# A two-half decoder trunk: where the second half's four delta heads get their buffers and their projections

## The chip, the cores and the metric

The kernel runs on one core of a Trainium2 chip. The metric is the device time of one execution in microseconds (us); less is better. Before the change three runs gave a median of 2281.3 us (2279.24 to 2283.44).

## What is computed

The input x is 1024 tokens of width 1024 in fp32. Two residual layers follow one another; after each mixer and after each MLP stands a layernorm of `alpha * x + result`. Cut to what matters here:

```python
def hybrid_mixer(x, w_in, ...):                       # layer 0
    proj = x @ w_in
    qa, ka, va, qkv_b, z, beta_logit, a_logit = split_cols(proj, HYB_SPLITS)
    o_a = sliding_window_attention(rope(qa), rope(ka), va, sinks)      # 8 heads of 64, 2 kv heads, window 128
    qb, kb, vb = split(silu(causal_dwconv(qkv_b, conv_w)))             # 4 delta heads of 128, 4 taps
    o_b = gated_delta_rule(l2_normalize(qb), l2_normalize(kb), vb, g, beta)   # chunks of 64, state carried
    o_b = o_b * rsqrt(mean(o_b ** 2) + eps) * norm_w * silu(z)
    return concat([o_a, o_b]) @ w_out
def recurrent_mixer(x, ...): ...                      # layer 1: conv, RG-LRU, gelu gate, two projections
def sqrelu_mlp(x, w1, w2): return relu(x @ w1) ** 2 @ w2
for layer in range(2):
    x = layer_norm(alpha * x + (hybrid_mixer, recurrent_mixer)[layer](x))
    x = layer_norm(alpha * x + sqrelu_mlp(x))
```

## The kernel before, in words

**Products.** A product of fp32 accuracy is made of three TensorE products of a faster 32-bit format: both operands are split into a high part h and a low part l, and `mm3` (L359) adds h·h, h·l and l·h in PSUM. A weight block of 128x1024 is loaded by SyncE's DMA queue into one of three `ws` buffers, its h is cast by ScalarE (every fifth by VectorE) into `wh`, and VectorE subtracts to get `wl` (`wblock`, L349; `split`, L343). Activations lie split in granules of 128x2048 (`gran`, a pool of 14); an `ActT` is the transposed activation of one half as four granules: quads 0 and 1 of h and of l.

**Halves and order.** The 1024 tokens are worked on as two halves c = 0 and c = 1 of 512 tokens. Each half is a generator `stream(c)` (L1329): hybrid mixer, output projection `hout` with layernorm (`mix_out`), MLP (`w1`, `w2`), recurrent mixer, MLP. The long weight products in it are the *fillers*: each `yield` releases three TensorE matmuls. The chains of short, dependent steps are *mixers*, generators too, put on a list by `spawn`: the delta heads (`head_mid`, L944), the attention blocks (`attn_preps`, `attention`), `delta_scalars`, layernorms, loads. The loop at L1355 writes TensorE's one fixed order while the program is built: a modelled clock says when a mixer's next inputs are there; if they are, its step comes next, otherwise three matmuls of a stream's filler. A generator that must wait for a buffer or a flag yields `BLOCK`. If no stream has a filler to give, the modelled clock is simply moved on, and the mixer's next step follows with nothing between. The other engines work in the order in which their instructions were issued at that build, one after the other.

**Buffers of the chains.** Besides granules there are rings of 128x512 tiles: `t` with 11, `s` with 10 and `f` with 4. A delta head keeps its q, k, v and its chain's tiles in one ring (`r`) until its end, and `need(r, n)` waits for n free tiles.

**The delta heads** are started in `hybrid` (L1246). `head_front` (L911) makes k, q and v of a head: product from `hin_fm` into PSUM, ScalarE copies it into an `f` tile beside three columns of the tokens before (`halo`), a four-tap convolution (`conv4`: one ScalarE step, three VectorE steps) and silu. `head_z` (L932) makes z, silu'd and split into quad 1 of `oT`. `head_mid` then runs the chain: transposes, Gram matrices, the inverse in levels of 32x32 matmuls, the scan over chunks, a norm, and the product with z into `oT`. In half c = 0 the heads take the rings t and s in turn, so two chains run at a time; in half c = 1 all four take ring t, one after the other, and each front waits for the ring. The z of a head is made behind the front of the next. Half 2's x is loaded (`load_x`) after the first two z of half 1. `q_proj` (L760) copies q into a granule of its own, which `attn_prep` (L796) reads; `mix_out` of half 1 keeps gamma and beta of its layernorm in four tiles of ring s, half 2 in ring t (`load_gb`, L438). `straight` (L553), one of the MLP's two ways to hold its hidden tiles, takes eight tiles of ring t or s.

In the profile L178 is the line through which all instructions of VectorE, ScalarE, GpSimd and the DMA queues go, L206 that of matmuls and L210 that of transposes; in the changed file they are L179, L207 and L211. `mm` are PSUM tiles of weight products, `mx` those of the chains' steps.

Of the kernel before, what the change touches and what calls it, by code (L numbers as in the profile page):

```python
# [13 lines left out]
ALU = mybir.AluOpType  # L14
# [15 lines left out]
FW = 528  # L30
LN_EPS = 1e-5
# [182 lines left out]
def trunk(ctx: ExitStack, tc, I, out):  # L214
# [223 lines left out]
    def load_gb(which, r):  # L438
        g = [ts(r) for _ in range(4)]
# [11 lines left out]
    def layernorm(yg, ls, which, r, yT, res, each=None):  # L451
        yield from need(r, 4)
# [12 lines left out]
        def norm(n, i):  # L465
# [8 lines left out]
            if (n, i) == halves[-1]:  # L474
                free(r, *g)
# [53 lines left out]
    def mlp(layer, c, yT, yg, ls, res, tail=False):  # L529
# [23 lines left out]
        def straight(e, done):  # L553
            j, i = divmod(e, 2)
            yield from wait(lambda: either(8))
            ring = either(8)
            own = [(ts(ring, F32R), ts(ring, F32R)) for _ in range(4)]
# [10 lines left out]
            for half in range(2):  # L568
# [13 lines left out]
                if half == 1:  # L582
                    free(ring, *(z for hl in own for z in hl))
                    if done:
                        res["n"] = NT
# [174 lines left out]
    def q_proj(c, x, st, oT):  # L760
        ps = yield from proj_tm([I["hin_q"][i] for i in range(4)], x, 512)
        st["qg"] = gran()
        for n in range(NT):
            oT.quad(0, n)
            S.copy(st["qg"][:, n * CH:(n + 1) * CH], ps[n])
# [30 lines left out]
    def attn_prep(c, n, st, tl, o):  # L796
        q, kr = v4(st["qg"][:, n * CH:(n + 1) * CH]), st["k"][n]
# [113 lines left out]
    def head_front(c, h, x, d, r):  # L911
        for j, name in enumerate("kqv"):
            yield from need(r, 1)
            yield from need("f", 2)
            raw, y, u = tl("f"), ts("f"), ts(r)
            ps = yield from proj_fm(I["hin_fm"][h * 4 + j], x)
            i = h * 3 + j
# [4 lines left out]
            S.copy(raw[:, 3:515], ps)  # L922
            if c == 0:
                S.copy(halo[:, i, :], raw[:, 512:515])
# [7 lines left out]
    def head_z(h, x, oT, d):  # L932
        yield from need("f")
        z = ts("f")
        ps = yield from proj_fm(I["hin_fm"][h * 4 + 3], x)
        S.activation(z, ps, AF.Tanh, scale=0.5)
        V.scalar_tensor_tensor(z, z, 1.0, ps, ALU.add, ALU.mult)
        S.copy(oT.h(4 + h), z)
        V.tensor_tensor(oT.l(4 + h), z, oT.h(4 + h), ALU.subtract)
        free("f", z)  # L940
# [3 lines left out]
    def head_mid(c, h, st, d, oT, r):  # L944
# [151 lines left out]
        yield from wait(lambda: "z" in d)  # L1096
# [6 lines left out]
        V.tensor_tensor(z, oT.h(4 + h), oT.l(4 + h), ALU.add)  # L1103
# [400 lines left out]
```

## Time and profile before

| | |
|---|---|
| median of three runs | 2281.3 us |
| profiled execution, its time | 2280.57 us |
| its span (first to last instruction) | 2278.7 us |
| granted TensorE clock, mean | 0.991 |
| TensorE busy | 2216.7 us |
| VectorE (DVE) busy | 1545.9 us |
| ScalarE (ACT) busy | 1049.1 us |
| moved by DMA | 332.22 MB |

The first layer's mixers of both halves lie in the first 500 us of the span; half 1's first MLP begins at about 463 us. The windows of the trace give, for a stretch of the span, the busy time of each engine, the granted clock (1.00 is full speed) and the share of time that the DMA engines were busy. The timeline gives single instructions; in brackets stands how long the engine had been idle before one, and whose instruction ended that.

### The profile page before, as it was taken

The numbers are of one execution on the slowest core, as the hardware profiler recorded it, in microseconds if no ns is written. First come the engines' busy times: TensorE is split into PE (matmuls) and PEld (weight loads), VectorE is DVE, ScalarE is ACT, GpSimd is POOL, SyncE is SP. The second block draws the span as 40 slices with busy tenths as digits, with TensorE's granted clock in tenths as the row PEclk, the third lists the DMA queues.
The fourth block names the chain that finished last, engine by engine and source line by source line (L and its number), as shares of the span: only waits on it lengthen the run. The fifth ranks groups of instructions, "written<-read, shape, count | busy, mean of one in ns | idle before, by whom it ended". The sixth has DMA issues, their size and how long they took to land.

```text
span 2278.7 us, 31897 instructions
## 1 busy us (share of the span) xinstructions
PE 2216.7 (97%) x12436; PEld 1790.4 (79%) x12436; DVE 1545.9 (68%) x2809; ACT 1049.1 (46%) x1874; POOL 28.9 (1%) x56
## 2 busy tenths in 40 slices
PE   8999989999999999999999999999999999999997
PEld 7767866778878887888888878878788887888886
DVE  7787684766645666596567898685565656776477
ACT  5465444434332344454344577373434444444442
POOL 0000000000000000000000000000000000000000
PEclk9999999999999999999999999999999999999999
DMA  4121221266778666677764343322533443454341
GB/s 165 61 78 39 94 67 45 74 175 178 216 213 225 196 211 200 210 241 229 226 216 149 128 138 105 136 79 97 180 107 121 139 148 123 155 166 148 120 163 69
DMA packets 87064, 332.22 MB, mean 146 GB/s; under 512 B 9600, under 2 KB 9984, under 8 KB 78720
## 3 DMA queue, kind: packets, MB, share of 16 engines
q1 hardware_dynamic: 73808, 275.32, 35.2%
q0 software_dynamic: 4608, 33.56, 7.8%
q10 hardware_dynamic: 8496, 21.30, 2.7%
q8 instruction: 97, 1.59, 0.3%
q14 instruction: 55, 0.45, 0.1%
HBM read 321.75 MB, written 75.50 MB: 174 GB/s over the span
## 4 chain that ended last, share of the span: by engine, by line
PE 85%; DVE 9%; ACT 3%; DMA 1%; issue 1%; ACTq 0%; DVEq 0%; SPq 0%
PE mm L206 66%; PE mx L206 17%; DVE g L178 3%; DVE wl L178 2%; PE mx L210 2%; DVE s L178 1%; DMA ws<-w 1%; ACT g L178 1%; ACT wh L178 1%; ACT s L178 1%; DVE t L178 1%; DVE f L178 1%; ACT f L178 0%; ACT t L178 0%; DVE lnw L178 0%
## 5 line engine op out<-in xcount | busy, mean ns | idle before, releaser
L206 PE MATMUL mm<-g,wh 128*128 128x512 f32 x2816 | 883.7, 395 | 3.6 <-DVE g L178 3.0
L178 DVE TENSOR_TENSOR wl<-ws,wh 128x1024 fp32r<-128x1024 f32 (+1 forms) x444 | 538.3, 1212 | 396.1 <-ACT wh L178 391.8
L178 ACT CAST wh<-ws 128x1024 fp32r<-128x1024 f32 (+1 forms) x356 | 371.5, 1044 | 705.8 <-PE mm L206 605.3
L206 PEld LDWEIGHTS mm<-g,wh 128*128 128x128 f32 x2816 | 521.6, 188 | 113.4 <-DVE g L178 5.1
L206 PE MATMUL mm<-g,wl 128*128 128x512 f32 x1408 | 549.5, 390 | 0.5 <-DVE wl L178 0.5
L206 PE MATMUL mm<-wh,s 128*128 128x512 f32 x1152 | 376.6, 393 | 0.7 <-DVE g L178 0.7
L206 PEld LDWEIGHTS mm<-g,wl 128*128 128x128 f32 x1408 | 264.7, 188 | 57.0 <-DVE wl L178 1.0
L206 PEld LDWEIGHTS mm<-wh,s 128*128 128x128 f32 x1152 | 216.3, 188 | 46.7 <-ACT s L178 1.1
L206 PE MATMUL mm<-wh,g 128*128 128x512 f32 (+1 forms) x768 | 239.3, 383 | 6.6 <-ACT wh L178 6.4
L206 PE MATMUL mm<-wl,s 128*128 128x512 f32 x576 | 224.3, 389 | 0.0
L206 PE MATMUL mx<-wh,s 128*128 128x512 f32 x576 | 187.8, 392 | 1.2 <-DVE s L178 1.2
L206 PEld LDWEIGHTS mm<-wh,g 128*128 128x128 f32 x768 | 143.0, 191 | 33.8 <-ACT wh L178 6.4
L178 ACT CAST s<-g 128x512 fp32r<-128x512 f32 x172 | 104.7, 622 | 105.2 <-PE mm L206 53.7
L178 DVE TENSOR_TENSOR s<-g,s 128x512 fp32r<-128x512 f32 x172 | 116.1, 685 | 44.7 <-ACT s L178 44.7
L206 PE MATMUL mm<-wl,g 128*128 128x512 f32 (+1 forms) x384 | 144.1, 375 | 0.2 <-DVE wl L178 0.2
L206 PEld LDWEIGHTS mx<-wh,s 128*128 128x128 f32 x576 | 108.1, 188 | 24.1 <-DVE s L178 2.0
L206 PEld LDWEIGHTS mm<-wl,s 128*128 128x128 f32 x576 | 108.3, 188 | 20.9
L206 PE MATMUL mx<-wl,s 128*128 128x512 f32 x288 | 112.1, 389 | 0.0
L178 DVE CAST wh<-ws 128x1024 fp32r<-128x1024 f32 x88 | 60.4, 686 | 73.0 <-PE mm L206 66.3
L178 DVE TENSOR_TENSOR g<-g,mm 128x512 f32<-128x512 f32 x136 | 89.1, 682 | 14.6 <-PE mm L206 14.2
L178 ACT ACTIVATE g<-mm 128x512 f32<-128x512 f32 x100 | 59.3, 593 | 73.0 <-PE mm L206 73.0
L206 PEld LDWEIGHTS mm<-wl,g 128*128 128x128 f32 x384 | 73.3, 191 | 11.7 <-DVE wl L178 0.6
(231 smaller groups left out, 2401.3 us busy)
## 6 DMA issues: line engine op xcount, KB each, us to landing
ws<-w SPq DMA_DIRECT2D x232, 512.0 KB, 3.3
ws<-t SPq DMA_DIRECT2D x96, 512.0 KB, 3.3
t<-w POOLq DMA_DIRECT2D x32, 1024.0 KB, 9.1
ws<-hin_fm SPq DMA_DIRECT2D x32, 512.0 KB, 3.3
t<-w SPq DMA_DIRECT2D x16, 1024.0 KB, 6.7
t<-t SPq DMA_DIRECT2D x16, 1024.0 KB, 6.5
ws<-rin SPq DMA_DIRECT2D x32, 512.0 KB, 3.3
ws<-hout SPq DMA_DIRECT2D x16, 512.0 KB, 3.4
```

Source lines behind the costliest of these rows:

```text
L178: r = f(*a, **k)
L206: ins = self.pe.matmul(out, lhsT, rhs, start=start, stop=stop, skip_group_check=fresh)
L210: return self._pe(self.pe.transpose(out, x, ident), out, [x], 0.00042 * 2 * out.shape[-1])
```

## The change

- `SHARED = (3,)`: head 3's k, q and v blocks, and the z blocks of all four heads, are multiplied with x of both halves at once (`proj_fm` with `also`), in half 1's stream; 25 blocks of `hin_fm` are loaded and split in place of 32. For heads 0 to 2 of half 2, k, q and v are made by `fronts` as fillers of stream 1.
- `park` copies such a raw product out of PSUM with ScalarE into a tile `r` (two buffers) and stores it with SyncE's queue in DRAM (`parked_i`, 128x512). `head_front` and `head_z` of half 2 load it from there into an `f` tile, once it is parked.
- The heads of half 2 take the rings t and s in turn and are a mixer of their own (`heads`, spawned), no part of the stream.
- z of half 1 goes unsplit into one granule `zg`; in half 2 it is split into `oT` as before. All four z come after the four fronts.
- `q_proj` of half 2 splits q into the quads of `oT`, and `attn_prep` adds h and l again; half 1 keeps its granule.
- gamma and beta of half 1's first layernorm take a granule in place of four s tiles; `straight` may take two granules where no ring has eight tiles.
- x of half 2 is loaded from the start of half 1 on, and freed when both halves have used it (`drop`).

```diff
+SHARED = (3,)
-    def proj_fm(src, x, bank=None):
+    def proj_fm(src, x, bank=None, also=None):
         wh, wl = wblock(src)
-        ps = (bank or mm_ps)()
+        xs = [x] if also is None else [x, also]
+        ps = [(bank or mm_ps)() for _ in xs]
         for k in range(KT):
             b, c = divmod(k, 4)
-            mm3(ps, wh[b][:, c * P:(c + 1) * P], wl[b][:, c * P:(c + 1) * P], x.h(k), x.l(k), k == 0, k == KT - 1)
-            if k < KT - 1:
-                yield
-        return ps
+            for i, z in enumerate(xs):
+                mm3(ps[i], wh[b][:, c * P:(c + 1) * P], wl[b][:, c * P:(c + 1) * P], z.h(k), z.l(k), k == 0, k == KT - 1)
+                if k < KT - 1 or z is not xs[-1]:
+                    yield
+        return ps[0] if also is None else ps
...
+            if c:
+                V.tensor_tensor(qs, *q, ALU.add)
+                q = qs
             rope(qs, q, 4, n, a, b)
...
+    def park(i, ps):
+        t = dpool.tile([P, CH], F32, name=f"parked_{i}", tag=f"parked_{i}")
+        o = clk.tile("r", 2, wpool.tile([P, 512], F32, tag="r", name=nm("r"), bufs=2))
+        S.copy(o, ps)
+        DS.dma_start(t, o)
+        parked[i] = t
...
     def head_front(c, h, x, d, r, also=None):
         for j, name in enumerate("kqv"):
+            i = h * 3 + j
+            b = h * 4 + j
+            yield from wait(lambda: c == 0 or b in parked)
             yield from need(r, 1)
             yield from need("f", 2)
             raw, y, u = tl("f"), ts("f"), ts(r)
-            ps = yield from proj_fm(I["hin_fm"][h * 4 + j], x)
-            i = h * 3 + j
+            if c:
+                DS.dma_start(raw[:, 3:515], parked[b])
+            else:
+                ps = yield from proj_fm(I["hin_fm"][b], x, also=also)
+                if also is not None:
+                    park(b, ps[1])
+                    ps = ps[0]
...
     def head_mid(c, h, st, d, oT, r):
-        yield from wait(lambda: "z" in d)
+        yield from wait(lambda: "z" in d and (("l", 1) in oT.g or rings["g"] >= 2))
+        oT.quad(1, 0)
...
+        def fronts(h):
+            for j in range(3):
+                ps = yield from proj_fm(I["hin_fm"][h * 4 + j], x)
+                park(h * 4 + j, ps)
+                yield UNIT
...
+        def heads():
+            for h in range(4):
+                if c == 0 and h in SHARED:
+                    yield from wait(lambda: "x" in sts[1])
+                yield from head_front(c, h, x, d[h], rs[h % 2], both if h in SHARED else None)
+                yield from wait(lambda: h - st.get("scan", 0) < 2)
+                spawn(head_mid(c, h, st, d[h], oT, rs[h % 2]))
+                if h == 0 and c == 0:
+                    yield from q()
+            if c:
+                yield from wait(lambda: "ln0" in sts[0])
+                yield from need("g", 2)
+                oT.quad(1, 0)
+            else:
+                yield from need("g", 1)
+                zg.append(gran())
+            for h in range(4):
+                yield from head_z(c, h, x, oT, d[h], both)
+        if c == 0:
+            yield from heads()
+            x.free()
+        else:
+            spawn((r if r is not UNIT else lambda: 0.0) for r in heads())
             yield from q()
+            yield UNIT
+            for h in range(1, 4):
+                if h not in SHARED:
+                    yield from fronts(h)
+        drop()
...
-        yield from hybrid(c, xT, oT, st[c], ("t", "s") if c == 0 else ("t",))
+        yield from hybrid(c, xT, oT, st[c], ("t", "s"))
         yield from mix_out(I["hout"], oT, lambda n: I["x"][c * CH + n * P:c * CH + (n + 1) * P, :], 0,
-                           "s" if c == 0 else "t", s, st[c]["t"], lambda: c == 0 or "m7" in sts[0])
+                           "g" if c == 0 else "t", s, st[c]["t"], lambda: c == 0 or "m7" in sts[0])
```

More of the change, by code (lines that the diff above doesn't have):

```diff
@@ L438, in load_gb @@
     def load_gb(which, r):
-        g = [ts(r) for _ in range(4)]
+        if r == "g":
+            q = gran()
+            g = [q[:, i * 512:(i + 1) * 512] for i in range(4)]
+        else:
+            g = [ts(r) for _ in range(4)]
         for i in range(4):
@@ L554, in straight @@
             j, i = divmod(e, 2)
-            yield from wait(lambda: either(8))
+            yield from wait(lambda: either(8) or rings["g"] >= 2)
             ring = either(8)
-            own = [(ts(ring, F32R), ts(ring, F32R)) for _ in range(4)]
+            if ring:
+                own = [(ts(ring, F32R), ts(ring, F32R)) for _ in range(4)]
+                held = [z for hl in own for z in hl]
+            else:
+                ring, held = "g", [gran(F32R) for _ in range(2)]
+                own = [tuple(z[:, i * 512:(i + 1) * 512] for z in held) for i in range(4)]
             for f in range(4):
@@ L1259, in q @@
         def q():
-            yield from need("g", 3)
+            yield from need("g", 3 - c)
             yield from q_proj(c, x, st, oT)
```

96 lines of the change are left out of this document (54 added, 42 removed).

## The prediction

> **What bounds the kernel now.** First the page: how full TensorE is, and whose chain ended last.
>
> ```profile
> span 2278.7 us, 31897 instructions
> ...
> PE 2216.7 (97%) x12436; PEld 1790.4 (79%) x12436; DVE 1545.9 (68%) x2809; ACT 1049.1 (46%) x1874; POOL 28.9 (1%) x56
> ...
> PE 85%; DVE 9%; ACT 3%; DMA 1%; issue 1%; ACTq 0%; DVEq 0%; SPq 0%
> ```
>
> TensorE is busy 97%, and the change leaves its matmuls alone in number, so all there is to win is its 2278.7 - 2216.7 = 62 us of idleness, and matmuls that ran slowly. Second the windows, which say where these lie; the columns are busy time and instructions of PE, PEld, DVE, ACT and POOL, then granted clock, DMA share and GB/s.
>
> ```profile
> 60.00:120.00 60.00, 57.62 (x823) 42.38 (x821) 42.75 (x130) 24.95 (x77) 0.10 (x1) 1.00 0.17 54
> 120.00:180.00 60.00, 55.49 (x331) 41.92 (x331) 52.14 (x164) 38.78 (x113) 0.51 (x5) 1.00 0.27 82
> 180.00:240.00 60.00, 57.80 (x809) 40.41 (x807) 43.82 (x121) 34.07 (x103) 0.00 (x0) 1.00 0.16 47
> 240.00:310.00 70.00, 68.97 (x482) 58.03 (x481) 51.97 (x172) 31.14 (x95) 0.00 (x0) 1.00 0.26 83
> 310.00:366.00 56.00, 45.05 (x465) 28.71 (x465) 32.61 (x100) 28.77 (x85) 0.00 (x0) 0.82 0.17 58
> 366.00:430.00 64.00, 64.00 (x297) 45.79 (x296) 32.34 (x79) 26.64 (x69) 0.00 (x0) 1.00 0.18 59
> 430.00:500.00 70.00, 66.09 (x572) 51.72 (x571) 53.36 (x130) 35.66 (x73) 1.75 (x2) 0.95 0.45 131
> ```
>
> One window stands out: from 310 to 366 us TensorE idles 56 - 45.05 = 10.95 us, and its clock is 0.82 where it is 1.00 around it. Third the timeline of TensorE there (start, duration, operation, in brackets the idle time before and its releaser); mx are steps of chains, mm are weight products, the fillers.
>
> ```profile
> 307.42 0.45 PE L206 MATMUL mx<-t 32*32 32x32 f32 x32
> 307.80 0.73 PE L206 MATMUL mm<-g,wh 128*128 128x512 f32 x2
> ...
> 308.60 0.62 PE L206 MATMUL mm<-g,wh 128*128 128x512 f32 x2
> ...
> 309.29 0.62 PE L206 MATMUL mm<-g,wh 128*128 128x512 f32 x2
> ...
> 316.79 0.45 PE L206 MATMUL mx<-t 32*32 32x32 f32 x32
> 318.07 0.45 PE L206 MATMUL mx<-t 32*32 32x32 f32 x32 [0.82 <-DVE t L178]
> 319.38 0.45 PE L206 MATMUL mx<-t 32*32 32x32 f32 x32 [0.86 <-DVE t L178]
> ...
> 323.53 1.97 PE L206 MATMUL mx<-g,vraw 128*64 128x512 f32 x2 [1.68 <-DVE g L178]
> ...
> 330.61 1.07 PE L206 MATMUL mx<-g,vraw 128*64 128x512 f32 x2 [0.40 <-DVE g L178]
> ...
> 340.91 1.08 PE L206 MATMUL mx<-t,t 64*64 64x64 f32 x8 [2.13 <-DVE asc L178]
> ...
> 360.54 1.16 PE L206 MATMUL mx<-kT,g 64*128 64x128 f32 x16
> ...
> 364.96 0.48 PE L206 MATMUL mm<-wh,g 128*128 128x512 f32 x1
> ```
>
> Up to 316.79 us fillers lie between chain steps and hide them; from there to 364.96 us, 48.2 us long, stands a bare run without one. A step of 0.45 us waits 0.82 us for DVE, and the same pair of 128x512 matmuls takes 1.97 us at one place and 1.07 at another. The idle and slow parts together: 10.95 + 0.18 x 45.05 = 19.1 us.
>
> **The change part by part.** (1) *The bare run.* Before, TensorE's order at its start (mm the last filler, mx_..<-t head 0's levels in half 2, mx<-csb and vraw the attention):
>
> ```order
> L206 MATMUL mm_3659<-g_2006,wh_3655 128x512
> L206 MATMUL mm_3659<-g_2005,wl_3656 128x512
> L206 MATMUL mx_3692<-t_3388 32x32 x16
> L206 MATMUL mx_3710<-t_3388 32x32 x16
> L206 MATMUL mx_3729<-t_3388 32x32 x16
> L210 MATMUL mx_3748<-csb,g_146 128x128 x2
> L210 MATMUL mx_3748<-csb,g_147 128x128 x2
> ```
>
> And in the changed kernel the same levels, between products of `hout`:
>
> ```order
> L207 MATMUL mm_486_3651<-wh_491_3657,g_106_756 128x512
> L207 MATMUL mx_493_3676<-t_464_3492 32x32 x16
> L207 MATMUL mm_487_3652<-wh_491_3657,g_105_755 128x512
> L207 MATMUL mm_487_3652<-wl_492_3658,g_105_755 128x512
> L207 MATMUL mm_487_3652<-wh_491_3657,g_106_756 128x512
> L207 MATMUL mm_488_3653<-wh_491_3657,g_105_755 128x512
> L207 MATMUL mm_488_3653<-wl_492_3658,g_105_755 128x512
> L207 MATMUL mm_488_3653<-wh_491_3657,g_106_756 128x512
> L207 MATMUL mm_489_3654<-wh_491_3657,g_105_755 128x512
> L207 MATMUL mm_489_3654<-wl_492_3658,g_105_755 128x512
> L207 MATMUL mm_489_3654<-wh_491_3657,g_106_756 128x512
> L207 MATMUL mx_494_3703<-t_464_3492 32x32 x16
> ```
>
> Nine fillers now lie between two levels: three start 0.69 us after the three before (308.60, 309.29), so nine take 2.1 us against a wait of 0.8 to 1.0. The bare run's loss goes: -19.1 us; at least -10.95, if the clock falls there as well.
>
> The row has a clock of 0.82 though its longest wait is 2.13 us. The Trainium skill's page "TensorE: Matmul & The Clock Gate" (Part 1: The HAM clock gate) says that the clock halves after an idle window of about 3.4 us; by that rule no slow clock should be here and the term would be 10.95 us. The row contradicts it, and I keep 19.1.
>
> (2) *The first layernorm of half 1.* Today it loses time at its transposes and the first `w1` product:
>
> ```profile
> 457.76 1.91 PE L210 MATMUL mx<-csb,g 128*128 128x128 f32 x16
> 461.92 1.71 PE L210 MATMUL mx<-csb,g 128*128 128x128 f32 x8 [2.25 <-DVE g L178]
> 463.30 0.80 PE L206 MATMUL mm<-g,wh 128*128 128x512 f32 x1
> 465.77 0.79 PE L206 MATMUL mm<-g,wh 128*128 128x512 f32 x1 [1.67 <-DVE g L178]
> ```
>
> With its window (70 - 66.09 = 3.9 idle, 0.05 x 66.09 = 3.3 slow) it costs 7.2 us. In the changed kernel the same place reads on TensorE (csb,g the transposes, kT attention scores, mm_4564 the last parked product of head 2, mm_4829 the first of `w1`):
>
> ```order
> L207 MATMUL mm_4564<-g_345,wl_4561 128x512
> L211 MATMUL mx_4731<-csb,g_3644 128x128 x4
> L211 MATMUL mx_4741<-csb,g_3644 128x128 x4
> L211 MATMUL mx_4751<-csb,g_3644 128x128 x4
> L211 MATMUL mx_4758<-csb,g_3644 128x128 x4
> L211 MATMUL mx_4786<-csb,g_3645 128x128 x4
> L211 MATMUL mx_4796<-csb,g_3645 128x128 x4
> L211 MATMUL mx_4806<-csb,g_3645 128x128 x4
> L211 MATMUL mx_4813<-csb,g_3645 128x128 x4
> L207 MATMUL mm_4829<-g_4694,wh_4825 128x512
> L207 MATMUL mm_4829<-g_4695,wh_4825 128x512
> L207 MATMUL mm_4829<-g_4694,wl_4826 128x512
> L207 MATMUL mx_4833<-kT_4184,g_146 128x128
> ```
>
> All eight transposes now come in one piece, and in DVE's order layernorm, attention of half 2 and the convolutions of heads 1 and 2 stand mixed. From the filler 123 before these transposes to the last split of the layernorm DVE has 136 instructions. The groups by form up to 715 us, the last column but two the mean ns:
>
> ```profile
> L178 DVE TENSOR_TENSOR wl<-ws,wh 128x1024 fp32r<-128x1024 f32 x82 | 100.2, 1222 | 55.0 <-ACT wh L178 53.9
> L178 DVE SCALAR_TENSOR_TENSOR f<-f,sm,f 128x512 f32<-128x512 f32 x72 | 53.4, 744 | 6.0 <-ACT f L178 5.3
> ...
> L178 DVE CUSTOM_DVE_ANT_0 g<-mx,csb 128x256 f32<-128x256 f32 x56 | 20.5, 419 | 1.8 <-PE mx L206 1.7
> ...
> L178 DVE TENSOR_TENSOR hsc<-hsc 128x4 f32<-128x4 f32 x80 | 12.6, 159 | 3.5 <-ACT t L178 1.8 <-ACT s L178 0.3
> ...
> L178 DVE TENSOR_TENSOR g<-mx,g 128x512 fp32r<-128x512 f32 x16 | 10.8, 684 | 10.8 <-ACT g L178 10.8
> ...
> L178 DVE TENSOR_TENSOR g<-g,s 128x512 f32<-128x512 f32 x14 | 9.2, 684 | 0.0
> ```
>
> 6 splits x 1.222 = 7.3; 17 convolution steps x 0.744 = 12.6; 14 layernorm halves and 9 splits x 0.684 = 15.7; 12 masks x 0.419 = 5.0; 29 small ones x 0.159 = 4.6; the other 49 take at most 0.684 each, 33.5 us, by kind about 20. Together about 65 us. TensorE has 123 fillers x 0.23 = 28 us there and 53 short rows, each between a score matmul (1.16 us for eight, 0.145) and four transposes (1.91 for sixteen matmuls, four such, 0.48): 8 to 25 us, by kind 17; together 45. So TensorE could wait 65 - 45 = 20 us if DVE arrived without any lead, and 7.2 if it is like today. I take the middle, 14: **-7.2 + 14 = +6.8**.
>
> (3) *Heads 1 and 2 of half 2 elsewhere* have three to six fillers (0.7 to 1.4 us) between steps, against a level's wait of 0.82 to 0.86: between 0 and +6, I take +2.
>
> (4) *Half 1.* Head 3's k, q, v and all z blocks serve both halves (seven loads and splits fewer), half 1's z isn't split, and the second products fill. Its windows from 60 to 240 us hold 2.38 + 4.51 + 2.20 = 9.1 us of idleness: between -4.5 and 0, I take -1.5. q's two additions more in half 2 fall under the count of (2).
>
> (5) *DRAM.* Sixteen products are copied by ACT, stored and loaded again through SP. SP's rows at heads 1 and 2 of half 2 (ws weight blocks, parked the stores, f<-parked the loads):
>
> ```order
> L179 DMA parked_4292<-r_4293 128x512
> L179 DMA ws_4823<-w_0 128x1024
> L179 DMA f_4296<-parked_4292 128x512
> L179 DMA parked_4373<-r_4374 128x512
> L179 DMA f_4377<-parked_4373 128x512
> L179 DMA parked_4419<-r_4420 128x512
> L179 DMA ws_4951<-w_0 128x1024
> L179 DMA ws_5017<-w_0 128x1024
> L179 DMA f_4423<-parked_4419 128x512
> ```
>
> ```profile
> L178 ACT ACTIVATE g<-mm 128x512 f32<-128x512 f32 x100 | 59.3, 593 | 73.0 <-PE mm L206 73.0
> ...
> ws<-hin_fm SPq DMA_DIRECT2D x32, 512.0 KB, 3.3
> ...
> out<-g SPq DMA_DIRECT2D x16, 256.0 KB, 2.1
> ```
>
> A load waits on SP for its store, and weight blocks queue behind it. One round trip is 0.6 + 2.1 + 3.3 = 6.0 us (a read of 512 KB as bound for 256). A block of `w1` behind it is needed some 120 fillers, 27 us, later: 0. DMA share there is 0.17 to 0.45: no contention.
>
> Sum: -19.1 + 6.8 + 2 - 1.5 = -11.8 us on the profiled execution's 2280.6, so 2268.8; the median of the runs is 0.7 higher, so **2269.5 us**.
>
> **The rivals.** *Nearly all is kept*: DVE enters the layernorm with a lead and loses 7.2 us as today, (3) costs nothing: -19.1 - 1.5 = -20.6, 2260.7 us. For it: DVE is busy only 32.34 of the 64 us after the bare run. Against: the 20 us counted in (2).
> *DVE takes it back*: it has no lead, 20 us in (2): -19.1 - 7.2 + 20 + 2 = -4.3, 2277.0 us, no change that can be told (0.2%, 4.6 us, is about what a measurement of this kernel can tell). For it: at 430 to 500 us DVE was busy 53.36 of 70 with one chain, and now has two. Against: today's loss there is 7.2.
> *The round trips stand in DVE's queue* and it ends slower. A convolution's first step waits on DVE for its load; behind it in the same queue stand the layernorm's splits, which `w1` waits for. If DVE has caught up when it comes there, it idles up to 6.0 us a product, for six of them, in a stretch where DVE is the bound. Against: with a backlog of DVE they are hidden. It decides from 4.3 + 4.6 = 9 us of such waits, two round trips; with three, 18 us on -4.3: 2295.
>
> **How the numbers follow.** The forecast 0.48, nearly all kept 0.18, taken back 0.19, round trips 0.15. Faster by over 0.2%: 0.66; within: 0.19; slower: 0.15. The range runs from a little beyond the kept case, 2256 (both waits of (4) and half of today's 7.2 gone as well), to 2286, halfway into the round trips' case.
>
> **What would show it.** Right: no stretch at head 0 of half 2 without fillers and the clock near 1.00 there; one hole of 10 to 18 us at the first transposes before `w1`, ended by DVE. The second rival: that hole near 20 us and DVE full before it. The third: DVE idle on DMA f<-parked. Wrong altogether: half 1's loss grows by more than 5 us, or weight splits waiting for DMA ws.

## The result, and the profile after

| | before | after |
|---|---|---|
| median of four runs each | 2280.27 us (2279.17 to 2283.44) | 2300.97 us (2299.31 to 2302.48) |
| span of the profiled execution | 2278.7 us | 2298.1 us |
| granted clock, mean | 0.991 | 0.988 |

After over before is 1.0088, with a 95% interval of 1.0071 to 1.0106: the change makes the kernel about 20 us slower. The forecast was 2269.5 us, in a range that ended at 2286: wrong in sign and outside the range.

The page of the changed kernel begins with its busy times; further down it gives the shares of the chain that ended last.

```profile
span 2298.1 us, 31959 instructions
...
PE 2225.6 (97%) x12436; PEld 1795.7 (78%) x12436; DVE 1540.1 (67%) x2801; ACT 1041.2 (45%) x1868; POOL 28.5 (1%) x56
...
PE 86%; DVE 7%; ACT 3%; DMA 2%; issue 1%; DVEq 0%; ACTq 0%; SPq 0%
PE mm L207 67%; PE mx L207 18%; DVE g L179 3%; PE mx L211 2%; DVE wl L179 1%; DVE s L179 1%; ACT g L179 1%; DVE f L179 1%; ACT s L179 1%; DMA f<-parked 1%; DMA ws<-xT 0%; ACT wh L179 0%; DMA ws<-w 0%; ACT f L179 0%; DMA parked<-r 0%
```

The matmuls are as many as before (12436) and VectorE, ScalarE and GpSimd are each a little less busy, yet the span is 19.4 us longer. DMA has gone from 1% to 2% of the chain, and beside the weight blocks (`ws<-w`) three kinds of transfer are named in it: loads of parked products, stores of them, and loads of x (`ws<-xT`). None of the three had a term above zero in the prediction.

Where the time lies, the windows say. First the changed kernel, then those windows of the kernel before that the prediction did not show (columns as there: busy time of PE, PEld, DVE, ACT, POOL, then granted clock, DMA share, GB/s).

```profile
0.00:60.00 60.00, 46.79 (x240) 40.64 (x241) 38.41 (x97) 30.06 (x76) 0.44 (x7) 0.94 0.56 188
60.00:310.00 250.00, 239.49 (x2302) 178.89 (x2301) 146.91 (x451) 107.66 (x316) 0.91 (x9) 0.98 0.15 50
310.00:366.00 56.00, 53.70 (x415) 44.39 (x414) 46.76 (x129) 23.52 (x73) 0.00 (x0) 1.00 0.37 128
366.00:430.00 64.00, 64.00 (x482) 51.02 (x481) 43.57 (x122) 21.77 (x51) 0.00 (x0) 1.00 0.28 91
430.00:560.00 130.00, 116.83 (x1119) 82.40 (x1118) 95.72 (x248) 69.89 (x185) 3.40 (x4) 0.95 0.50 143
560.00:760.00 200.00, 198.39 (x1222) 159.10 (x1222) 126.48 (x297) 80.45 (x176) 8.40 (x12) 1.00 0.70 206
760.00:1480.00 720.00, 713.79 (x3174) 587.08 (x3173) 502.88 (x692) 351.09 (x503) 15.38 (x24) 1.00 0.60 188
1480.00:1560.00 80.00, 72.39 (x315) 58.74 (x314) 60.02 (x91) 52.08 (x79) 0.00 (x0) 0.91 0.25 84
```

```profile
0.00:60.00 60.00, 53.38 (x285) 46.41 (x286) 43.07 (x111) 31.63 (x79) 0.75 (x10) 1.00 0.46 161
60.00:310.00 250.00, 239.89 (x2442) 182.74 (x2440) 190.68 (x585) 128.93 (x387) 0.61 (x6) 1.00 0.22 67
...
430.00:560.00 130.00, 126.09 (x967) 100.84 (x966) 93.89 (x225) 60.70 (x136) 4.23 (x5) 0.97 0.54 155
560.00:760.00 200.00, 200.00 (x1389) 160.90 (x1388) 110.77 (x241) 62.26 (x121) 9.55 (x13) 1.00 0.75 216
760.00:1480.00 720.00, 711.86 (x3166) 585.63 (x3165) 519.05 (x732) 364.00 (x523) 13.77 (x22) 1.00 0.58 183
1480.00:1560.00 80.00, 74.63 (x335) 60.68 (x334) 59.66 (x81) 51.08 (x81) 0.00 (x0) 0.98 0.26 86
```

Busy time times granted clock is the work that TensorE got done, in us at full speed; idle time and slow clock are taken out of it together. The table gives it for the kernel before and, for the others, how much more or less they did in the same window (each figure rounded to a tenth before it is subtracted; the last three columns are experiments that come below):

| window | before | after minus before | h_before_x_early | d_same_products | dks4_equal_products |
|---|---|---|---|---|---|
| 0 to 60 | 53.4 | -9.4 | -11.3 | -0.1 | -0.3 |
| 60 to 310 | 239.9 | -5.2 | -16.1 | +4.2 | +4.2 |
| 310 to 430 | 100.9 | +16.8 | +0.9 | +9.5 | +13.4 |
| 430 to 560 | 122.3 | -11.3 | +0.4 | -30.1 | +3.1 |
| 560 to 760 | 200.0 | -1.6 | 0.0 | -1.4 | -3.4 |
| 760 to 1480 | 711.9 | +1.9 | +1.5 | +1.4 | -13.9 |
| 1480 to 1560 | 73.1 | -7.2 | -1.3 | -7.3 | +2.3 |
| sum | | -16.0 | -25.9 | -23.8 | +5.4 |
| its span minus before's | | +19.4 | +22.8 | +21.7 | -5.5 |

Each sum has the size of its span's difference; the rest is what the clock's second digit leaves (0.005 of 720 us is 3.6 us in the longest window). By 60 us the changed kernel and a_no_load, b_two_hops and c_ln_light of below, whose orders are still the same on every engine there, have done 44.0, 41.6, 41.1 and 41.5 us: a difference of up to 3 us in one window of single profiles says nothing. So four places matter. The bare run gained 16.8 us, as forecast. The start lost 9.4 + 5.2 = 14.6, half 1's first layernorm 11.3, and a place in the second layer 7.2.

**The start.** TensorE in the changed kernel stands still for 6.44 us at the delta scalars' cumulative sum; the kernel before has no wait there.

```profile
39.15 1.04 PE L207 MATMUL mx<-dsc,csb 128*128 128x16 f32 x4 [6.44 <-DVE dsc L179]
```

The chain that leads to it (start, duration, piece) goes through loads of half 2's x, one after the other:

```profile
18.02 3.87 DMA ws<-xT
...
23.89 3.86 DMA ws<-xT
...
29.83 3.65 DMA ws<-xT
...
34.15 1.29 DVE g L179 x2
...
39.01 0.10 DVE dsc L179
```

Each load is followed by a split on ScalarE and VectorE; `dsc`, the small steps of the decay scalars, stand between the splits in VectorE's fixed order, and so wait for DMAs that have nothing to do with them. The bracket names VectorE; the chain shows that a DMA held VectorE up.

**The layernorm of half 1.** The chain from 430 us on:

```profile
430.64 0.48 ACT r L179
431.14 2.01 DMA parked<-r
...
433.57 3.38 DMA parked<-r
437.01 3.46 DMA f<-parked
440.58 0.73 ACT f L179
...
450.34 0.59 ACT r L179
450.94 2.34 DMA parked<-r
453.29 4.98 DMA f<-parked
458.36 0.73 ACT f L179
```

Two passages through DRAM lie on this chain. The second is one product's round trip: 8.0 us from ScalarE's copy out of PSUM to ScalarE's first convolution step (450.34 to 458.36). The first, 9.9 us (430.64 to 440.58), holds two products: the store at its head is that of the product before, whose load waits for it in SP's queue, and the next store stands behind that load. The product convolved at 440.58 was copied out at 432.91, 7.7 us earlier. From 459.11 to 477.96 the chain is VectorE's alone: it had waited 2.40 us for ScalarE's step at 458.36, and from 459 to 478 us it is busy 18.79 of 19 us.

TensorE idles 13.2 us of the 130 there, in pieces. The longest stands before transposes of head 1 of half 2 (`csb,s`); the hole of 10 to 18 us at the transposes before `w1` (`csb,g`), which the prediction named as its sign, isn't there:

```profile
435.89 0.63 PE L211 MATMUL mx<-csb,s 128*128 128x128 f32 x4 [3.78 <-DVE hsc L179]
...
470.76 3.58 PE L211 MATMUL mx<-csb,g 128*128 128x128 f32 x16 [1.68 <-DVE g L179]
...
476.56 0.50 PE L207 MATMUL mm<-g,wh 128*128 128x512 f32 x1 [1.71 <-DVE g L179]
```

**The second layer.** In its mixer one chain step waits 6.30 us for VectorE:

```profile
1497.86 1.11 PE L211 MATMUL mx<-csb,g 128*128 128x128 f32 x4 [6.30 <-DVE g L179]
```

The diff does not touch that mixer. TensorE's order there differs all the same, presumably because the clock modelled at the build arrives with other values. Which versions have this wait is told at the last experiment.

### The profile page after: what moved, and what is told of

Same layout as the page of the kernel before. It is cut to its first block, busy times and chain, and to the rows that moved or that the text cites. A ratio compares the mean times of both kernels' runs of the same rounds, so it can differ in the third digit from the quotient of the medians.

```text
span 2298.1 us, 31959 instructions
## 1 busy us (share of the span) xinstructions
PE 2225.6 (97%) x12436; PEld 1795.7 (78%) x12436; DVE 1540.1 (67%) x2801; ACT 1041.2 (45%) x1868; POOL 28.5 (1%) x56
## 4 chain that ended last, share of the span: by engine, by line
PE 86%; DVE 7%; ACT 3%; DMA 2%; issue 1%; DVEq 0%; ACTq 0%; SPq 0%
PE mm L207 67%; PE mx L207 18%; DVE g L179 3%; PE mx L211 2%; DVE wl L179 1%; DVE s L179 1%; ACT g L179 1%; DVE f L179 1%; ACT s L179 1%; DMA f<-parked 1%; DMA ws<-xT 0%; ACT wh L179 0%; DMA ws<-w 0%; ACT f L179 0%; DMA parked<-r 0%
## 5 line engine op out<-in xcount | busy, mean ns | idle before, releaser
L179 DVE TENSOR_TENSOR wl<-ws,wh 128x1024 fp32r<-128x1024 f32 (+1 forms) x437 | 529.6, 1212 | 375.9 <-ACT wh L179 371.0
L179 ACT CAST wh<-ws 128x1024 fp32r<-128x1024 f32 (+1 forms) x350 | 364.8, 1043 | 656.1 <-PE mm L207 567.2
L207 PE MATMUL mm<-wh,g 128*128 128x512 f32 (+1 forms) x896 | 284.0, 387 | 7.6 <-ACT wh L179 6.5
L207 PE MATMUL mm<-wh,s 128*128 128x512 f32 x896 | 287.5, 390 | 1.4 <-DVE g L179 1.4
L207 PEld LDWEIGHTS mm<-wh,g 128*128 128x128 f32 x896 | 167.0, 191 | 39.7 <-ACT wh L179 6.5
L207 PEld LDWEIGHTS mm<-wh,s 128*128 128x128 f32 x896 | 168.2, 188 | 37.1 <-DVE g L179 2.3
L207 PE MATMUL mm<-wl,s 128*128 128x512 f32 x448 | 174.3, 389 | 0.0
L207 PE MATMUL mm<-wl,g 128*128 128x512 f32 (+1 forms) x448 | 169.7, 379 | 0.3 <-DVE wl L179 0.3
L207 PEld LDWEIGHTS mm<-wl,s 128*128 128x128 f32 x448 | 84.1, 188 | 17.2
L179 DVE TENSOR_TENSOR g<-g,mm 128x512 f32<-128x512 f32 x136 | 89.3, 683 | 11.4 <-PE mm L207 10.9
L207 PEld LDWEIGHTS mm<-wl,g 128*128 128x128 f32 x448 | 85.7, 191 | 13.5 <-DVE wl L179 0.6
```

The source lines that it names most:

```text
L179: r = f(*a, **k)
L207: ins = self.pe.matmul(out, lhsT, rhs, start=start, stop=stop, skip_group_check=fresh)
```

## The experiments

Theories at the outset: **TRIP**, the round trips of heads 1 and 2 of half 2 lie on the path; **DVE**, VectorE has too much work at the layernorm, as term (2) said; **START**, loading half 2's x from the start delays half 1. Later: **CROWD**, half 2's chains run in the layernorm's place; **MEET**, the layernorm meets half 2's attention; **MASK** against **KEPT**, whether what late loading of x wins early is given back at the layernorm or stays. All ratios are to the kernel before, with their 95% interval; after's is 1.0088 [1.0071, 1.0106].

### a_no_load, b_two_hops, c_ln_light, d_x_late: one cost at a time

```diff
 a_no_load, in head_front of half 2
+                if h in (1, 2):
+                    nc.gpsimd.memset(raw[:, 3:515], 0.25)
+                    ...
+                else:
+                    DS.dma_start(raw[:, 3:515], parked[b])
```

> Leaves out the six loads of heads 1 and 2 of half 2 from DRAM (their convolutions run on a constant that GpSimd writes; the stores stay; TensorE's order is row for row that of the changed kernel). Theory TRIP (store and load lie on the chain that TensorE waits for, at 431 to 441 and 451 to 458 us of the changed kernel's trace): 8 to 15 us faster than the changed kernel, the hole before the transposes at 435.9 us gone. Theory DVE (in that stretch VectorE simply has more work than TensorE): 0 to 2 us faster.

```diff
 b_two_hops, in head_front of half 2
+                if h in (1, 2):
+                    hop = dpool.tile([P, CH], F32, name=f"hop_{b}", tag=f"hop_{b}")
+                    nc.sync.dma_start(hop, parked[b])
+                    nc.sync.dma_start(raw[:, 3:515], hop)
```

> Sends the same six products through DRAM twice (store, copy from DRAM to DRAM, load), TensorE's order unchanged. TRIP: each of the two trips on the chain grows by one more transfer of 256 KB, 2 to 3.5 us each: 4 to 8 us slower than the changed kernel. DVE: 0 to 1 us slower.

```diff
 c_ln_light, in layernorm
+                if r == "g":
+                    ...
+                else:
                     V.tensor_tensor(a, a, g[i], ALU.mult)
                     V.tensor_tensor(a, a, g[2 + i], ALU.add)
```

> Leaves out the multiplication by gamma and the addition of beta for seven of the eight half tiles of half 1's first layernorm (14 VectorE instructions, 14 x 0.61 us from start to start = 8.5 us less for VectorE), TensorE's order unchanged. TRIP: 0 to 2 us faster than the changed kernel. DVE: 6 to 9 us faster.

```diff
 d_x_late
-            spawn(load_x(1, xTs[1]))        # in stream, at the start of half 1
                 if h == 0 and c == 0:
                     yield from q()
+                    spawn(load_x(1, xTs[1]))
```

> Half 2's x is loaded after half 1's q product instead of from the start on; the planner's order changes behind it. Theory START (the four loads and sixteen splits of x in the first 40 us hold up the decay scalars): the wait of 6.4 us and the slow clock at 33 to 45 us go, 7 to 10 us faster there, and 4 to 10 us faster in all. Rival: the same splits only fall into the dense stretch of half 1's heads and come back there: the start is faster, the whole within 3 us.

Measured: a_no_load 2294.16 us, 1.0059 [1.0044, 1.0074]; b_two_hops 2307.38, 1.0117 [1.0102, 1.0132]; c_ln_light 2302.15, 1.0094 [1.0079, 1.0109]; d_x_late 2293.81, 1.0063 [1.0046, 1.0080]. TensorE's order in a, b and c is, row for row, that of the changed kernel. VectorE's and ScalarE's is not: it differs in places, from 361 us on in a, from 421 us in c and from 425 us in b, until about 510 us. So these runs carry some reordering beside the cost that they change. The window from 430 to 560 us, of a, b and c in that order:

```profile
430.00:560.00 130.00, 121.61 (x1180) 86.45 (x1179) 88.35 (x247) 69.32 (x186) 3.40 (x4) 0.99 0.45 131
```

```profile
430.00:560.00 130.00, 112.14 (x1077) 79.18 (x1076) 94.11 (x242) 69.36 (x186) 3.34 (x4) 0.92 0.48 144
```

```profile
430.00:560.00 130.00, 116.37 (x1112) 82.43 (x1110) 90.04 (x225) 69.20 (x181) 3.40 (x4) 0.92 0.48 142
```

Without the six loads TensorE does 121.61 x 0.99 = 120.4 us of work there, with them 111.0, with one hop more 103.2. The kernel follows: 6.8 us faster without, 6.4 slower with a further hop. That is TRIP's way in both, within its 4 to 8 us for b, but less than its 8 to 15 for a: about 1.1 us a product. TensorE's idle time in the window is 8.4 us without the loads, 13.2 with them and 17.9 with one hop more. The wait of 3.78 us before head 1's transposes is gone without the loads and grows to 5.98 with the hop; it is 5.38 in c_ln_light too, whose trips are those of the changed kernel, so this one hole alone proves nothing. The waits of that stretch name the engine (total, times, longest us), first in the changed kernel, then with one hop more; without the loads ScalarE has no such wait:

```profile
ACT f L179 <- DMA f<-parked: 8.6, 4, 2.7
```

```profile
ACT f L179 <- DMA f<-hop: 7.4, 4, 2.7
```

(Of the 8.6 us, 1.5 are head 3's product; with the hop that one waits 1.7.) It is ScalarE that waits, since the convolution's first step is its own. Its own waits hardly grow with the hop, though, while TensorE's do: what a trip costs is passed on through the engines' orders, and the traces don't split it by product. Behind the first of these steps (440.58) stand in ScalarE's order the copy of the next product out of PSUM (441.81), four steps of a delta chain (445.31) and the cast of a weight block (449.38).

DVE, as term (2) had counted it, falls: c_ln_light takes 14 of VectorE's layernorm instructions away, 14 x 0.684 = 9.6 us, and gains nothing where DVE had said 6 to 9 us; the window has 5.7 us less VectorE work and no more TensorE work than after. But these 14 run from 421 to 431 us in the changed kernel, ahead of the stretch from 459 to 478 us in which VectorE is full. Of that stretch c says little: VectorE is busy 17.62 of the same 19 us in it. (The memset gives GpSimd six instructions more, so a's 6.8 us carries that too.)

d_x_late gains 7.2 us, within START's 4 to 10, but its plan has 24 matmuls fewer (12412). In before's chain 26 fillers take 5.90 us, 0.227 each, so 24 are 5.4 us. It had to be asked again, below.

### e_direct, k5_hold: take heads 1 and 2 out of the way

```diff
 e_direct: no trip for heads 1 and 2 of half 2; product and convolution in the stream
-            if c:
+            if c and h not in (1, 2):
                 DS.dma_start(raw[:, 3:515], parked[b])
...
+            if c and h in (1, 2):
+                S.copy(raw[:, 3:515], ps)
...
+            mixer(heads((0,), False))
             yield from q()
...
+            yield from heads((1, 2), False)
+            mixer(heads((3,)))
```

> Heads 1 and 2 of half 2 take k, q and v straight from PSUM into their tiles, in the stream, as every head of the kernel before did; both rings, head 0's and head 3's parked products and all z stay as changed; the reference is computed in full. TRIP: as much faster than the changed kernel as without the six loads, 5 to 8 us. Rival: fronts that wait for a ring stop the stream again, TensorE gets bare stretches, and the gain is under 3 us.

```diff
 k5_hold: heads 1 to 3 of half 2 wait until half 1's first layernorm is done and the
 head before in their ring has ended; z head by head
+                if c and h:
+                    yield from wait(lambda: st.get("mids", 0) >= h - 1)
+                    yield from wait(lambda: phase[0] >= 1)
                 yield from head_front(...)
...
+                if c and h:
+                    if h == 1:
+                        yield from wait(lambda: "ln0" in sts[0])
+                        yield from need("g", 2)
+                        oT.quad(1, 0)
+                        yield from head_z(c, 0, x, oT, d[0], both)
+                    yield from head_z(c, h, x, oT, d[h], both)
```

> Heads 1 to 3 of half 2 start only when half 1's first layernorm is done (so that w1 products lie between their steps), a head's front waits until the head before it in its ring has ended, and z of half 2 is loaded head by head; everything else as changed. Theory CROWD (the round trips cost only because layernorm and heads 1 and 2 stand together with few fillers between): the loss at 430 to 510 us (18.8 us above the work of TensorE itself, against 7.7 in the kernel before) falls to 8 to 11, 8 to 11 us faster than the changed kernel. Rival: the layernorm alone is as slow, the wait comes back behind it: under 3 us.

Measured: e_direct 2312.40 us, 1.0150 [1.0132, 1.0168]; k5_hold 2310.58, 1.0138 [1.0122, 1.0155]. Both are slower than the changed kernel, by 11.4 and 9.6 us, where TRIP had said 5 to 8 us faster and CROWD 8 to 11. The stretch from 420 to 480 us of e_direct, then of k5_hold:

```profile
420.00:480.00 60.00, 45.89 (x210) 33.95 (x209) 58.03 (x137) 41.31 (x110) 0.00 (x0) 0.88 0.19 63
```

```profile
420.00:480.00 60.00, 48.89 (x219) 35.35 (x218) 43.01 (x111) 36.61 (x88) 0.00 (x0) 0.83 0.33 112
```

In e_direct VectorE is busy 58.03 of 60 us: here VectorE does become the bound. In k5_hold VectorE has room, and TensorE still does only 48.89 x 0.83 = 40.6 us of work. Holding the heads alone is no cure; 24 matmuls more (12460 in all), 5.4 us, explain part of its loss over the changed kernel.

### dk5_late_hold, dk6_late_hold_g: both at once

dk5_late_hold is k5_hold with the line moved as in d_x_late. dk6_late_hold_g besides forbids half 1's first MLP the rings:

```diff
-            yield from wait(lambda: either(8) or rings["g"] >= 2)
-            ring = either(8)
+            big = lambda: either(8) if layer or c or sts[1].get("mids") == 4 else None
+            yield from wait(lambda: big() or rings["g"] >= 2)
+            ring = big()
```

> The held heads together with half 2's x loaded after half 1's q product. START and CROWD together: the first 310 us as in the run with x late alone (no wait at 33 us), and the hole of 34 us that this run had at half 1's layernorm falls to 10 or less: 2266 to 2274 us, faster than the kernel before. Rival: with x late the hole comes from half 2's attention and head 0, which are not held: 2285 us or more.

> As the run before, and the first MLP of half 1 holds its hidden tiles in granules until all heads of half 2 have ended, so that a ring is not taken from these heads. START and CROWD: within 4 us of the run before; if heads 2 and 3 waited for their ring there, up to 6 us faster.

Measured: dk5_late_hold 2279.74 us, 1.0001 [0.9992, 1.0011], with 24 matmuls more than before; dk6_late_hold_g 2281.97, 1.0008 [0.9998, 1.0018], with as many as before. dk5 lies between its theory (2266 to 2274 us) and the rival (2285 or more). Late x is worth 2310.58 - 2279.74 = 30.8 us on top of the hold, four times its 7.2 alone (and those shrink to 0.4 with equal matmuls, below). So the two costs are not a sum: one hides behind the other. Which MLP form the rings allow is worth nothing that could be told here.

### ka_attn_held, dka_all_held, dkb_all_held_g: the attention as well

```diff
 ka_attn_held is the changed kernel with this; dka_all_held is dk5_late_hold with it;
 dkb_all_held_g is dk6_late_hold_g with it (in attn_preps)
+        yield from wait(lambda: c == 0 or phase[0] >= 1)
```

> The changed kernel with one wait more: half 2's attention starts only when half 1's first layernorm is done. Theory MEET (holding the heads did not help because half 2's attention, with sixteen short exponentials a block on ScalarE, meets the layernorm there as well): the loss between 420 and 560 us falls by 6 to 10 us, and the whole by as much. Theory TRIP alone: heads 1 and 2 and their round trips are still there: within 2 us of the changed kernel.

> Half 2's x late, its heads 1 to 3 and its attention held until half 1's first layernorm is done, z loaded head by head. START and MEET together: the hole of 15 us that the run with late x and held heads had at this layernorm falls to 8 or less, as in the kernel before (7.7): 2270 to 2275 us, faster than the kernel before by 0.2 to 0.45%. Rival: the attention only comes back behind the layernorm among the heads: 2278 to 2283 us.

> As the run before, and the first MLP of half 1 holds its hidden tiles in granules until half 2's heads have ended, so that heads, attention and w1 products come closer together. MEET: within 4 us of the run before; a stretch of 30 us more with chains under few fillers could cost 2 to 5 us.

Measured: ka_attn_held 2297.65 us, 1.0078 [1.0063, 1.0093]; dka_all_held 2277.21, 0.9992 [0.9982, 1.0001]; dkb_all_held_g 2286.84, 1.0028 [1.0016, 1.0041]. The window from 430 to 560 us of ka_attn_held, dk5_late_hold and dka_all_held:

```profile
430.00:560.00 130.00, 119.70 (x1157) 90.33 (x1158) 103.20 (x263) 68.31 (x180) 3.41 (x4) 0.96 0.49 145
```

```profile
430.00:560.00 130.00, 121.35 (x831) 90.37 (x830) 95.26 (x219) 64.55 (x149) 4.38 (x5) 0.93 0.55 168
```

```profile
430.00:560.00 130.00, 126.42 (x894) 92.02 (x894) 96.24 (x231) 74.74 (x191) 5.92 (x7) 0.97 0.69 195
```

Work done there: 111.0 us in the changed kernel, 114.9 with the attention held, 112.9 with late x and the heads held, 122.6 with all three, which is what the kernel before does (122.3). MEET alone is worth 3.3 us of time and with the others 2.5, with intervals that overlap in both cases: likely, but not shown by the times alone; MEET had said 6 to 10 us alone and 2270 to 2275 us for dka_all_held, and both fell short. dkb_all_held_g has 24 matmuls fewer than dka_all_held and is 9.6 us slower, where within 4 us was expected: the MLP's form that spares products doesn't pay when the buffers alone choose it.

### d_same_products, h_before_x_early: what late x is worth

```diff
 d_same_products: d_x_late, and in mlp (the loop that chooses straight blocks)
-        while e < 8 and not ((c == 1 or sts[1].get("op", -1) >= layer) and ...
+        while e < 8 and not ((c or layer or e >= 4) and (c == 1 or sts[1].get("op", -1) >= layer) and ...

 h_before_x_early: the kernel before, with the load moved from behind head_z(1) of half 1 to its start
+            spawn(load_x(1, xTs[1]))
...
-                spawn(load_x(1, xTs[1]))
```

> Half 2's x late, as in the run of that name, but with as many products as the changed kernel: that run's planner had turned to the cheaper form of the second MLP product two steps earlier and so had 24 filler matmuls less (24 x 0.227 = 5.4 us). Reading MASK (the late x gained about 19 us in the first 310 us and lost as much at half 1's layernorm, and the 5.7 us by which that run was faster were the 24 matmuls): 2297 to 2302 us, no faster than the changed kernel by more than 3. Reading KEPT (the late x kept part of its gain): 2291 to 2296 us.

> The kernel before with one line moved: half 2's x is loaded from the start, as in the changed kernel, and nothing else. START (the loads and splits of x hold up the decay scalars whatever follows): the wait before the decay scalars' matmul at 33 us appears, 6 to 7 us, and 8 to 10 us are lost by 66 us. Rival (it takes the shared products as well): under 3 us lost by 66 us. In all 8 us or more slower than before, by what the other order of half 2 adds.

Measured: d_same_products 2300.53 us, 1.0086 [1.0071, 1.0101], with as many matmuls as the changed kernel and the same time. MASK holds: d_x_late's 7.2 us were its 24 matmuls and little else. What late x wins by 310 us and what becomes of it, in d_same_products:

```profile
0.00:60.00 60.00, 53.29 (x280) 46.45 (x281) 39.86 (x107) 28.39 (x72) 0.44 (x7) 1.00 0.46 161
60.00:310.00 250.00, 244.08 (x2372) 185.27 (x2371) 158.11 (x475) 115.48 (x344) 0.90 (x9) 1.00 0.19 65
...
430.00:560.00 130.00, 103.57 (x914) 74.80 (x914) 97.38 (x272) 70.28 (x185) 1.95 (x4) 0.89 0.34 104
```

By 310 us it has done 297.4 us of work where the changed kernel has done 278.7: the 14.6 us of the start come back, and 4.1 more, on which term (4) had counted. Then the layernorm loses 30.1 us against before, where the changed kernel lost 11.3. Two waits of its transposes there, from the timeline:

```profile
497.16 1.11 PE L211 MATMUL mx<-csb,g 128*128 128x128 f32 x4 [3.65 <-DVE g L179]
...
513.74 1.11 PE L211 MATMUL mx<-csb,g 128*128 128x128 f32 x4 [6.32 <-DVE g L179]
```

h_before_x_early 2303.54 us, 1.0105 [1.0089, 1.0120]: one line of the change, made alone, costs the kernel before 23 us (START had said 8 or more; the planner's order changes with it). Its hole is the same one, and its loss lies where the changed kernel's does, 11.3 us by 60 us and 16.1 more by 310 (table above):

```profile
38.99 1.03 PE L206 MATMUL mx<-dsc,csb 128*128 128x16 f32 x4 [7.36 <-DVE dsc L178]
```

START is shown, then, from both sides.

### dks4_equal_products, dks2_fewer_products: a version that keeps the gain

Both are dka_all_held, with half 1's first MLP allowed the sparing form from block 4, or 2, on, so that dks4 has the 12436 matmuls of before and dks2 24 fewer than dks4.

```diff
-        while e < 8 and not ((c == 1 or sts[1].get("op", -1) >= layer) and ...
+        while e < 8 and not ((c == 1 or sts[1].get("op", -1) >= layer or (layer == 0 and e >= 4)) and ...
```

> x late, half 2's heads 1 to 3 and attention held until half 1's layernorm is done, and as many products as before and changed kernel (the held version had 24 filler matmuls more, 5.4 us). The theory (bare run gone, start as before, layernorm as before): 2271 to 2274 us, 0.2 to 0.35% faster than the kernel before. Rival: the half 2 stretch behind the layernorm eats it: 2276 us or more.

> The same with the cheaper form of the second MLP product two steps earlier still: 24 filler matmuls less than the kernel before. The theory: 5.4 us faster than the run with equal products, 2265 to 2269 us. Rival: its sums of weights are not ready in time or its hidden tiles wait for a ring: no faster than the run with equal products.

Measured: dks4_equal_products 2276.65 us over 11 runs, 0.9984 [0.9975, 0.9993]; dks2_fewer_products 2276.53 over 12, 0.9984 [0.9975, 0.9993]. Both are faster than either kernel, by 3.7 us against before and some 24 against the change; both came out at their rival's time, not at the theory's 2271 to 2274 and 2265 to 2269 us. Of dks4:

```profile
430.00:560.00 130.00, 127.98 (x900) 93.29 (x901) 95.68 (x233) 76.09 (x194) 6.43 (x7) 0.98 0.70 199
...
760.00:1480.00 720.00, 705.10 (x3129) 578.41 (x3128) 532.47 (x777) 365.85 (x527) 12.93 (x21) 0.99 0.55 179
```

```profile
430.83 3.77 PE L211 MATMUL mx<-csb,g 128*128 128x128 f32 x16 [4.70 <-DVE g L179]
...
1471.76 1.11 PE L211 MATMUL mx<-csb,g 128*128 128x128 f32 x4 [6.31 <-DVE g L179]
```

By 560 us dks4 has done 20.4 us more work than before (the first four rows of the table): the bare run's gain and the shared blocks' gain are both there. One wait of 4.70 us is left at the layernorm. From 560 to 1560 us it gives 15.0 back, so that only 5.5 us of span are won. The trace shows where: the second layer's wait is the changed kernel's, 6.31 us at 1471.76, and nearly all of the 13.9 us is lost from 1360 to 1480 us (110.41 x 0.96 = 106.0 us of work, against 119.74 before). From 761.82 us on, TensorE's order in dks4 is row for row that of the changed kernel from 787.72 us on. So dks4 mends the first layer and leaves the second as the change made it.

That wait is in all twelve versions of the changed kernel, the changed kernel itself among them, with 12436 or 12412 matmuls (6.29 to 6.31 us each time). It is in none of the three with 12460 (k5_hold, dk5_late_hold, dka_all_held), nor in the kernel before or h_before_x_early. dka_all_held and dks4 differ only in the MLP's sparing form: dks4 has 24 matmuls fewer, 5.4 us, and is 0.6 us faster. So the wait comes with that form, in versions of the change. How the form brings it about was not tried, nor why dks2's 24 matmuls less than dks4's bring nothing.

## Why the prediction was wrong, point by point

| term | forecast | measured in the windows |
|---|---|---|
| (1) bare run | -19.1 | -16.8 |
| (2) and (3) half 1's layernorm, heads 1 and 2 | +6.8 + 2 | +11.3 |
| (4) half 1, up to 310 us | -1.5 | +14.6 |
| (5) DRAM | 0 | in the row of (2) and (3) |
| second layer, 1480 to 1560 us | no term | +7.2 |
| 560 to 1480 us | no term | -0.3 |
| sum | -11.8 | +16.0 (span +19.4) |

- **(1) was right,** 16.8 us of 19.1. With fillers between head 0's levels the clock is 1.00 from 310 to 366 us and the idle time 2.3 us. That the slow clock would go with the idle time was right too.
- **(2) and (3) had about the right size for a wrong reason,** 11.3 us for 8.8, which is luck. The working counted VectorE's instructions and set them against TensorE's; c_ln_light took 9.6 us of them out and nothing moved, and where a hole of 10 to 18 us was to show it, no wait is longer than 1.71 us. What a_no_load and b_two_hops do move is the delay of a chain: copy, store, load, first step. The third rival had this mechanism, but on VectorE, at 6.0 us a product; the wait stands on ScalarE, and six products cost 6.8 us together. That this rival's 2295 us is the nearest number to 2300.97 is luck too, since most of the loss lies where it had none. ScalarE's order was never looked at for what is queued behind that step.
- **(4) is the step that failed:** of the 27.8 us between the two sums it has 16.1, the second layer 7.2, (2) with (3) 2.5 and (1) 2.3. It read the idle time of half 1 and asked how much of it the shared blocks would remove; the diff's moved line, x of half 2 loaded "from the start of half 1 on", got no price. Moving a step means moving every instruction that it issues: loads of x, and behind each the splits on ScalarE and VectorE, in the stretch where the delta scalars' small steps need VectorE. The sign was the other way by 16 us. The prediction's own test for this, "half 1's loss grows by more than 5 us", is what came true. The gain that (4) did forecast exists: d_same_products has it, 4.1 us by 310 us.
- **(5) asked the wrong question.** It asked whether weight blocks behind the trips would be late; they were not: no load of weights stands among the chain's longest pieces from 425 to 480 us. It did not ask who waits for the product itself. A product is made right before its use, so nothing lies between store and load to hide them. The Trainium skill's page "DMA: Bandwidth & Descriptors" (Anatomy of one DMA — SWDGE (gpsimd) path) has a fixed part of some 2 us in a transfer, most of it the receipt of the write. That is said of another queue, and no run here separates a fixed part. On SyncE's queue the trace shows, from 430 to 480 us, a median of 2.0 us for a store of 256 KB and 3.0 for a load, and on the chain 2.0 to 3.4 and 3.5 to 5.0, one after the other. So the trip's size, 6.0 us, was read about rightly (7.7 and 8.0 on the chain).
- **The second layer had no term.** An order planned by a modelled clock changes far from the edit. The wait of 6.30 us behind these 7.2 us is there with the late load (d_same_products) and with all held (dks4_equal_products), and gone only in the versions with 12460 matmuls; what in the plan makes it stays open.
- **The range.** With (4) at its bound of -4.5 and half of the 7.2 us gone, the kept case comes to 2254.1 us, not the 2256 given as the lower end. Nothing hangs on it.

**Where the gain went.** It was won, 16.8 us, and taken back before it and behind it. Undoing the early load alone gains nothing (d_same_products), presumably since half 1 then comes to its layernorm earlier and waits there for work that has not come earlier. Holding back half 2's heads alone loses (k5_hold); holding its attention alone gains at most a few us (ka_attn_held, 3.3). The early load, the heads and the attention together settle the first layer (dka_all_held, dks4_equal_products). The hold takes TRIP away as well: in dka_all_held heads 1 and 2's last raw product is stored at 428.24 us and the first one is loaded at 438.60, so these runs don't tell the crowd from the trips. That the three share one place is shown (late x alone 0.4 us, on top of the hold 30.8); how each one's share divides is not, and as the parts do not add, it may have no answer.

## What to carry to other kernels

Price a moved `spawn` or load like new work: list what it issues on each engine, and which small steps of another chain now stand behind it in that engine's fixed order. In a kernel whose order is planned at its build, compare variants only with the number of matmuls beside the time, and look at every stage in busy time times clock: a gain of 20 us in one stage can be gone two stages on. A value that goes through DRAM costs nothing only if something lies between its store and its use; ask who waits for the value, not only who queues behind the transfer.

## What the runs showed of the hardware

- The granted clock fell in stretches of many short waits: 0.82 from 310 to 366 us of the kernel before, whose longest wait is 2.13 us; 0.89 from 430 to 560 us in d_same_products, with waits up to 6.32 us; 0.83 from 420 to 480 us in k5_hold, up to 4.22 us. The slow clock is a good part of each loss: in d_same_products 11% of 103.57 us, 11.4 us, beside 26.4 us of idleness.
- One further copy from DRAM to DRAM of 256 KB in each of six chains cost 6.4 us in all, about 1.1 us each: much less than a transfer's 2.0 to 5.0 us, so most of each was still hidden.
